# Layer 1's input projection as four pairs of blocks with seven products each, their weights prepared in layer 0

## The chip, the cores and the metric

The kernel runs on one core of one Trainium2 chip. The metric is the device time of one execution in microseconds. Five engines work side by side, each on its own queue in a fixed order: TensorE (PE, with its weight loads shown as PEld), VectorE (DVE), ScalarE (ACT), GpSimd (POOL) and SyncE (SP), which here issues nearly all transfers (DMA).

## The reference, cut to what is computed

Two layers over x of 1024 tokens by 1024 channels, all in float32:

```python
for l in range(DEPTH):
    h = rmsnorm(x, attn_norm[l])
    proj = h @ w_in[l]                       # 1024 x 1952
    (c_q, c_kv, k_r, g_b, g_c, u_conv, u_pool, q_sw, k_sw, v_sw) = split(proj)
    y_a = mla_attention(c_q, c_kv, k_r, ...)         # causal, 4 heads, rotary key
    y_b = short_gated_conv(g_b, g_c, u_conv, ...)    # g_b * conv3(g_c * u)
    y_c = multiscale_pool(u_pool, ...)
    y_d = swa_sink_attention(q_sw, k_sw, v_sw, ...)  # window 128
    x = x + groupnorm([y_a, y_b, y_c, y_d]) @ w_o[l]
    gate, up = split(rmsnorm(x, ffn_norm[l]) @ w_gate_up[l])
    x = x + (silu(gate) * up) @ w_down[l]
return rmsnorm(x, final_norm)
```

## The kernel before

**Layout.** Channels lie on the 128 partitions and tokens along the free side, in two halves of 512 (t = 0 and 1). The channels of x make NK = 8 slices of 128. `w_in` is cut into blocks of 128 output columns: 2, 3 and 0 are the window attention's k, v and first q, 1 its second q, 4 to 9 the convolution's u, c and b for two channel groups, 10 to 12 the latent queries and keys, 13 and 14 the pool. A narrow block for the rotary key comes by itself.

**Arithmetic.** Each float32 operand is split into a high part (rounded by a cast on ScalarE, `split`, L286, or L218 for weights) and a low part (the remainder, on VectorE, L287 or L219). A product of two such numbers takes three matmuls, `mm3` (L275): high x high, high x low, low x high. A matmul is 128 x 128 by 128 x 512.

**Stages of a layer.** Input projection and mixers, attention and output projection, gate-up, down projection. In layer 0 the products of the down projection run from 808.6 us of the span to about 1021, and then layer 1's input projection begins. Gate-up and the down projection already use a scheme of seven products: a product of 2 x 2 blocks is made of seven block products instead of eight, from sums of the blocks. For the weights of the down projection those sums are made during gate-up by `dn_sums` (L164), which loads w_down, adds and stores to the DRAM tensor `qd`. The down projection has 28 units (seven products times four), each of 11 x 3 = 33 matmuls. For a unit the weights (`dn_raw`, L1455) are loaded from `in_w_dn` or `qd`, two pieces of 1024 and 384 columns, and split (`dn_weights`); for each of the seven products the activations (`dn_acts_raw`, L1472 and L1475) are loaded from `ad` and split. `evac` (L1642) adds a unit's sums onto x, which is loaded from `xr`, and `done` splits x times the next layer's gain into `hh`, which feeds the next input projection, and stores x to `xs`.

**Input projection.** `project` takes the next block's weights (`weights`: load L210, then the split) and makes for each half of the tokens 8 slices x 3 = 24 matmuls. The result is multiplied with r, the reciprocal norm of each token, when it is taken from PSUM (L360 and others). In layer 1 blocks 2, 3 and 0 come first.

**Memory and order.** Nearly all tiles live in N_U = 47 slots of two halves of 128 x 512, handed out in order; a tile `u_7577` is the 7577th one made, and a load into a slot waits until the readers of the slot's last tile are done. The order of each engine's queue is made by `order_engines` when the program is built: a table of numbers, MOVED, shifts each step's rank, and `arrange` then lists the steps. The engines keep that order on the chip. SP's transfers wait in the same way, one behind the other.

Of the kernel before, what the change touches and what calls it, by code (L numbers as in the profile page):

```python
# [18 lines left out]
P = 128  # L19
# [24 lines left out]
WARM = 10  # L44

# [70 lines left out]
def trunk_kernel(ctx: ExitStack, tc: tile.TileContext, ins, out):  # L116
# [26 lines left out]
    nffn = cpool.tile([P, L * NK], F32, name="nffn")  # L143
    act.preload_act_table_set("natural_log_exp_and_others")
# [6 lines left out]
    qd = dpool.tile([4, P, NK // 2 * NG * P], F32, name="qd")  # L151

    def dn_sums(l):
# [15 lines left out]

    PS_BUFS = {"mm": 2, "s": 3, "t": 2, "pv": 1}  # L170
# [6 lines left out]
        "dc": deque(["t", "t", "mm", "mm"]),  # L177
    }
# [14 lines left out]
    ring = deque()  # L193

    def ring_next():

        while len(ring) >= 2:
            ring_drop()
        ring.append((R.pair(), R.pair()))
        return ring[-1]  # L200

# [19 lines left out]

    def rope_weights(l):
# [12 lines left out]
    stream, fetched = deque(), deque()  # L235
# [4 lines left out]
    def expect_layer(l):  # L240
        for m in ((2, 3, 0) if l else ()) + (4, 5, 6, 1, 13, 14, 10, 11, 12, None, 7, 8, 9):
            if m is None:
                expect(rope_weights, l)
            else:
# [4 lines left out]
    def ahead():  # L249
        if stream and not fetched:  # L250
            f, args = stream.popleft()
            fetched.append(f(*args))
# [108 lines left out]

    def pcol(l, c, rows=slice(0, P)):
        return par[rows, l * PC_N + c : l * PC_N + c + 1]
# [80 lines left out]

    last_silu = None
    for l in range(L):
        if l == 0:
            expect_layer(0)
        sums = dn_sums(l)

# [17 lines left out]
        def project():  # L468
# [3 lines left out]
            return pp  # L472
# [12 lines left out]
        def swa_q(m, pp):  # L485
            for t in range(2):
                f = tmp()
                dve.scalar_tensor_tensor(
                    out=f, in0=pp[t], scalar=0.125, in1=r_of(t), op0=ALU.mult, op1=ALU.mult
                )  # L490
# [9 lines left out]
                )  # L500

        if l == 0:
# [6 lines left out]
            pk = [pk0, proj(wk, 1)]  # L509
            pv_ = [pv0, proj(wv, 1, "s")]  # L510
            enter_norm(0)
            pq = [pq0, proj(w, 1, "t")]
            enter_norm(1)
            dve.tensor_copy(e_r, cst[:, CC_E : CC_E + P])
            for i in range(L):
                for o, c, n in ((nsink, PC_SINK, 8), (nffn, PC_FFN, NK)):
# [7 lines left out]
        else:  # L524
            wk = take()
            pk = [proj(wk, 0, "s")]
            wv = take()
            pv_ = [proj(wv, 0, "s")]
            pk.append(proj(wk, 1))
            pv_.append(proj(wv, 1, "s"))  # L530
            w = take()
            pq = [proj(w, 0, "s"), proj(w, 1, "t")]
        ahead()
        kk = [[R.pair(), R.pair()] for _ in range(2)]
        for t in range(2):
            f = tmp()
            mul_to(f, pk[t], r_of(t))
            for g, own, oth in ((0, hd, tl), (1, tl, hd)):
# [4 lines left out]
                dve.tensor_tensor(out=k2[oth], in0=f[own], in1=rd(k1[own]), op=ALU.subtract)  # L543
        vs = [[R.half(), R.half()] for _ in range(2)]
        for t in range(2):
            f = tmp()
            mul_to(f, pv_[t], r_of(t))
# [12 lines left out]

        swa_q(0, pq)
# [151 lines left out]
        def conv(ct):  # L713

            z = F.pair()
            pp = project()
            for t in range(2):
                mul_to(F.ap(z + t), pp[t], r_of(t))
            yield
            pp = project()  # L720
            for t in range(2):
                f = tmp()
                mul_to(f, pp[t], r_of(t))
                mul_to(F.ap(z + t), F.ap(z + t), f)
            ac = F.pair()
# [14 lines left out]
            pp = project()  # L740
            for t in range(2):
                f = tmp()
                mul_to(f, pp[t], r_of(t))
                mul_to(F.ap(ac + t), F.ap(ac + t), f)
            y["b"][ct] = [ac, ac + 1]
            yield

        for _ in conv(0):
            swa_some(3)
        swa_q(1, project())  # L750
# [8 lines left out]
        nextp = project()  # L759
        for ct in range(2):  # L760
            pp = nextp
            u, a, b = F.pair(), F.pair(), F.pair()
            uf, af, bf = F.ap2(u), F.ap2(a), F.ap2(b)
            for t in range(2):
                mul_to(F.ap(u + t), pp[t], r_of(t))
            nextp = project()
# [51 lines left out]
        for m in range(2):  # L818
            pp = project() if m else nextp
            for t in range(2):  # L820
                f = tmp()
                mul_to(f, pp[t], r_of(t))
# [6 lines left out]
        pp = project()  # L829
        for t in range(2):  # L830
            s = F.half()
            mul_to(F.ap(s), pp[t], r_of(t))
# [302 lines left out]
        def minus(o, a, b):  # L1135
            dve.scalar_tensor_tensor(
                out=o, in0=a, scalar=-1.0, in1=b, op0=ALU.mult, op1=ALU.subtract
            )

# [106 lines left out]
        def product(p, w, b, start=True, stop=True, again=False):  # L1246
            terms = []
            for j, hl in enumerate(b):
                ks = slice(j * P, (j + 1) * P)
                terms.append((w[0][:, ks], w[1][:, ks], R.ap(hl[0]), R.ap(hl[1])))  # L1250
            mm3(p, terms, start, stop, again)

        def onto(p, w, b):

            product(p, w, b, False, True, True)

# [28 lines left out]
        for n, (h, t) in enumerate(steps):  # L1285
# [28 lines left out]
            if n == 6:  # L1314
# [12 lines left out]
                for k in range(2):  # L1327
                    src = ins["w_o"][l, 4 * k : 4 * k + 4, :, : 2 * P]
# [57 lines left out]

        def neg_mul(o, a, b):
            dve.scalar_tensor_tensor(
                out=o, in0=a, scalar=-1.0, in1=b, op0=ALU.mult, op1=ALU.mult
            )  # L1390
# [140 lines left out]
        for f in range(NPL, NFF):  # L1531
# [12 lines left out]
            if not end:  # L1544
                next(sums, None)
            gate = w.gate
# [73 lines left out]
        def done(d, t):  # L1620
# [7 lines left out]
            if not last:  # L1628
                F.free(x[d][t])

# [24 lines left out]
        for n, (c, m) in enumerate(units):  # L1655
            if n < 5:
                for _ in range(3):
                    next(sums, None)
            if n + 2 < len(units):
# [12 lines left out]
            w = wq.popleft()  # L1672
            i = n // NM
# [27 lines left out]
            elif c == B22:  # L1701
                done(2 * m, 1)
                if m == 0:
                    expect_layer(l + 1)
                    ahead()
# [81 lines left out]
DRAM_TILES = {"xs", "xp", "xr", "qd", "out"} | {f"ad{n}" for n in range(7)}  # L1787
BUFS = {"ps_mm": 2, "ps_s": 3, "ps_t": 2, "ps_pv": 1, "te": 2, "tn": 3, "tp": 3, "vraw": 2, "vhi": 2, "vlo": 2, "sm1": 16, "sm4": 16, "sm8": 16, "sm16": 2}
# [764 lines left out]
```

## Time and profile before

| | |
|---|---|
| three runs | 2051.62, 2052.42, 2052.92 us; median 2052.42 |
| span of the profiled execution, first to last instruction | 2050.3 us, 2.1 below that median |
| mean granted TensorE clock | 0.998 |
| PE, PEld, DVE, ACT, POOL busy | 2034.3, 1675.7, 1599.7, 981.9, 7.9 us |
| transfers | 289.74 MB, mean 141 GB/s |

A time of its own for the profiled execution is not listed beside its span. Rows of groups read: line, engine, operation, output and inputs, shapes, count, then busy time and mean duration of one in ns, then the idle time before it and what ended that. Rows of waits read: who, for whom, total us, times, longest. Rows of stretches: start and end in us, length, busy time and count of each engine, granted clock, share of the 16 transfer engines, GB/s. Rows of transfers: kind, count, size, median us from issue to landing.

### The profile page before, as it was taken

The numbers are of one execution on the slowest core, as the hardware profiler recorded it, in microseconds if no ns is written. First come the engines' busy times: TensorE is split into PE (matmuls) and PEld (weight loads), VectorE is DVE, ScalarE is ACT, GpSimd is POOL, SyncE is SP. The second block draws the span as 40 slices with busy tenths as digits, with TensorE's granted clock in tenths as the row PEclk, the third lists the DMA queues.
The fourth block names the chain that finished last, engine by engine and source line by source line (L and its number), as shares of the span: only waits on it lengthen the run. The fifth ranks groups of instructions, "written<-read, shape, count | busy, mean of one in ns | idle before, by whom it ended". The sixth has DMA issues, their size and how long they took to land. (4 is left out here: it accounts for less than half of the span.)

```text
span 2050.3 us, 26022 instructions
## 1 busy us (share of the span) xinstructions
PE 2034.3 (99%) x9418; PEld 1675.7 (82%) x9418; DVE 1599.7 (78%) x2742; ACT 981.9 (48%) x1713; POOL 7.9 (0%) x38
## 2 busy tenths in 40 slices
PE   9999999999999999999999999999999999999997
PEld 7887888888878888888888878877888888888887
DVE  7889988998778887556566898889987877876555
ACT  6447666653333335344443576657433333354342
POOL 0000000000000000000000000000000000000000
PEclk9999999999999999999999999999999999999999
DMA  5020223355445547766411102142564544487552
GB/s 182 24 73 21 74 84 111 113 190 176 161 143 186 172 154 232 240 236 221 139 37 44 47 22 93 57 146 101 175 203 151 179 160 146 167 295 242 172 195 86
DMA packets 149249, 289.74 MB, mean 141 GB/s; under 512 B 12672, under 2 KB 72064, under 8 KB 149120
## 3 DMA queue, kind: packets, MB, share of 16 engines
q1 hardware_dynamic: 148976, 288.03, 41.8%
q8 instruction: 74, 1.21, 0.2%
q14 instruction: 55, 0.45, 0.1%
q10 hardware_dynamic: 144, 0.05, 0.0%
HBM read 204.67 MB, written 83.36 MB: 140 GB/s over the span
## 5 line engine op out<-in xcount | busy, mean ns | idle before, releaser
L275 PE MATMUL ps_mm<-u,u 128*128 128x512 f32 (+1 forms) x3376 | 858.6, 389 | 0.3 <-DVE u L287 0.2
L275 PEld LDWEIGHTS ps_mm<-u,u 128*128 128x128 f32 x3376 | 617.0, 188 | 130.0 <-issue 5.9
L275 PE MATMUL ps_s<-u,u 128*128 128x512 f32 x2666 | 686.0, 390 | 2.4 <-DVE u L287 2.3
L275 PEld LDWEIGHTS ps_s<-u,u 128*128 128x128 f32 x2666 | 499.4, 188 | 109.6 <-DVE u L287 3.2
L286 ACT CAST u<-u 128x1024 fp32r<-128x1024 f32 (+2 forms) x385 | 334.7, 891 | 451.9 <-PE ps_mm L275 92.5
L287 DVE TENSOR_TENSOR u<-u,u 128x1024 fp32r<-128x1024 f32 (+2 forms) x385 | 387.6, 1023 | 161.3 <-ACT u L286 134.6
L275 PE MATMUL ps_t<-u,u 128*128 128x512 f32 (+1 forms) x1122 | 287.5, 379 | 1.0 <-DVE u L1642 1.0
L275 PEld LDWEIGHTS ps_t<-u,u 128*128 128x128 f32 x1122 | 203.5, 188 | 42.6 <-issue 1.7
L275 PE MATMUL ps_pv<-u,u 128*128 128x512 f32 x744 | 214.7, 390 | 0.5 <-ACT u L286 0.5
L275 PEld LDWEIGHTS ps_pv<-u,u 128*128 128x128 f32 x744 | 139.4, 188 | 30.4 <-ACT u L286 0.9
L289 ACT ACTIVATE u<-u,par 128x512 fp32r<-128x512 f32 x100 | 69.0, 717 | 40.5 <-DVE u L360 14.0
L1394 ACT ACTIVATE tp<-tp 128x512 f32<-128x512 f32 x84 | 52.8, 631 | 71.5 <-DVE tp L360 71.4
L164 DVE TENSOR_TENSOR u<-u 128x256 f32<-128x256 f32 x176 | 73.4, 421 | 14.9 <-DMA u<-in_w_dn 12.7
L286 ACT CAST u<-ps_t 128x512 fp32r<-128x512 f32 (+3 forms) x128 | 60.9, 501 | 50.2 <-PE ps_t L1036 28.0
L287 DVE TENSOR_TENSOR u<-ps_t,u 128x512 fp32r<-128x512 f32 (+3 forms) x128 | 71.7, 576 | 13.9 <-ACT u L286 12.7
L1262 ACT COPY tn<-ps_s 128x512 f32<-128x512 f32 x64 | 37.4, 584 | 79.5 <-PE ps_s L275 77.3
L290 DVE SCALAR_TENSOR_TENSOR u<-u,par,u 128x512 fp32r<-128x512 f32 x100 | 72.5, 746 | 3.1 <-ACT u L289 3.0
L321 ACT ACTIVATE tn<-u 128x512 f32<-128x512 f32 (+1 forms) x93 | 52.9, 592 | 35.4 <-DVE u L1642 25.7
L1395 DVE TENSOR_TENSOR tp<-tp,u 128x512 f32<-128x512 f32 x84 | 57.2, 686 | 11.8 <-ACT tp L1394 11.6
L219 DVE TENSOR_TENSOR u<-u,u 128x1024 fp32r<-128x1024 f32 (+1 forms) x43 | 48.1, 1119 | 16.0 <-PE ps_mm L275 6.4
L218 ACT CAST u<-u 128x1024 fp32r<-128x1024 f32 (+1 forms) x43 | 41.8, 971 | 39.0 <-DMA u<-in_w_in 26.7
L360 DVE TENSOR_TENSOR tp<-tp,u 128x512 f32<-128x512 f32 x84 | 57.3, 685 | 0.5
(196 smaller groups left out, 2007.3 us busy)
## 6 DMA issues: line engine op xcount, KB each, us to landing
u<-in_w_gu SPq DMA_DIRECT2D x88, 512.0 KB, 3.9
ad<-u SPq DMA_DIRECT2D x154, 256.0 KB, 2.1
u<-ad SPq DMA_DIRECT2D x70, 512.0 KB, 5.0
u<-in_w_dn SPq DMA_DIRECT2D x68, 512.0 KB, 3.7
qd<-u SPq DMA_DIRECT2D x44, 512.0 KB, 3.2
u<-qd SPq DMA_DIRECT2D x32, 512.0 KB, 5.2
u<-in_w_in SPq DMA_DIRECT2D x27, 512.0 KB, 3.5
u<-in_xT SPq DMA_DIRECT2D x32, 256.0 KB, 5.0
```

What stands on the lines that cost most here:

```text
L164: dve.tensor_tensor(out=o, in0=o, in1=u, op=ALU.add)
L218: act.copy(hi[:, :n], raw[:, :n])
L219: dve.tensor_tensor(out=lo[:, :n], in0=raw[:, :n], in1=rd(hi[:, :n]), op=ALU.subtract)
L275: pe.matmul(o, w, r, start=start and k == 0 and i == 0, stop=stop and k == n - 1 and i == 2, skip_group_check=again,)
L286: act.copy(hi, f)
L287: dve.tensor_tensor(out=lo, in0=f, in1=rd(hi), op=ALU.subtract)
L289: act.activation(hi, f, AF.Copy, scale=gain)
L290: dve.scalar_tensor_tensor(out=lo, in0=f, scalar=gain, in1=rd(hi), op0=ALU.mult, op1=ALU.subtract)
L321: act.activation(q, f, AF.Square)
L360: dve.tensor_tensor(out=o, in0=a, in1=b, op=ALU.mult)
L1394: last_silu = act.activation(g, g, AF.Silu)
L1395: dve.tensor_tensor(out=g, in0=g, in1=r, op=ALU.mult)
```

## The change

**Pairs.** In layer 1 the blocks (2, 3), (0, 5), (4, 6) and (1, 13) are worked as pairs. With the slices of x taken as even and odd (four each), the halves of the tokens and the two blocks of a pair, one pair is a 2 x 2 by 2 x 2 product, made of seven products of 4 slices x 3 = 12 matmuls each: A11 with x's even slices of half 0 (B11), A12 with the odd ones (B21), and S2, S1, S3, S4 and A22 with N2, N1, T3, T4 and B22. `in_round` runs each of the seven for all four pairs before the next, with new VectorE additions (L622, L643, L649) and ScalarE copies (L608) of the partial sums.

**Combinations of x.** `in_combine` makes N1, N2, T3 and T4 for each of four pairs of slices and splits them. It runs in the last quarter of layer 0's down projection, product B22, and needs x again, which is read back from `xs` (`again`, L1887).

**Weights.** The 15 block weights of layer 1 and its w_o are no longer loaded and split in layer 1. In layer 0 `pre_fast` loads the pairs' weights (`in_w_is`, laid out by the host), makes S1 to S4, splits all seven and stores both parts to `fw`; this runs in units 5 to 22 of the down projection. `pre_plain` does the same for the other seven blocks and w_o, without sums, to `pw`: seven sources in gate-up, ten in the down projection. In layer 1 both parts are loaded from there (`fast_weights`, `pre_weights`).

**Mixers.** The convolution takes u as it is and multiplies with the square of r; block 13 and block 5 or 6 are taken from PSUM or their sums earlier; a pair's second block comes with a negative sign.

**Order.** MOVED is new throughout.

```diff
+FAST = ((2, 3), (0, 5), (4, 6), (1, 13))
+PLAIN = (14, 10, 11, 12, 7, 8, 9)
+    fw = [dpool.tile([2, 7, P, HT], F32, name=f"fw{n}") for n in range(len(FAST))]
+    pw = [dpool.tile([2, P, D], F32, name=f"pw{n}") for n in range(N_PRE)]
+    def pre_fast():
+        n = HT // 2
+        for p in range(len(FAST)):
+            for c in range(0, HT, n):
+                cols = slice(c, c + n)
+                def put(k, v, first, m):
+                    v = v[:, : m * n].rearrange("p (b n) -> p b n", b=m)
+                    sp.dma_start(fw[p][k, first : first + m, :, cols].rearrange("b p n -> p b n"), v)
+                i, j = F.pair(), F.pair()
+                raw, lo = F.ap2(i), F.ap2(j)
+                v = raw.rearrange("p (b n) -> p b n", b=4)
+                sp.dma_start(v, ins["w_is"][p, :, :, cols].rearrange("b p n -> p b n"))
+                yield
+                h, hi = parted(raw[:, : 3 * n], lo[:, : 3 * n])
+                put(0, hi, A11, 3)
+                put(1, lo, A11, 3)
...
+                for o, u in ((b22, b21), (b21, b11), (b11, b22), (b12, b11)):
+                    dve.tensor_tensor(out=o, in0=o, in1=u, op=ALU.add)
+                yield
+                h, hi = parted(raw, raw)
+                put(0, hi, S2, 4)
+                put(1, raw, S2, 4)
...
+    def pre_plain():
+        src = [(ins["w_in"][1, m], D) for m in PLAIN]
+        src += [(ins["w_o"][1, d, :, 2 * P :], 6 * P) for d in range(NK)]
...
+        for o, (w, n) in zip(pw, src):
+            i = F.pair()
+            raw = F.ap2(i)[:, :n]
+            sp.dma_start(raw..., w)
+            yield
+            h, hi = parted(raw, raw)
+            sp.dma_start(o[0, :, :n], hi)
+            sp.dma_start(o[1, :, :n], raw)
...
+        if l:
+            for k in (A11, A12, S2, S1, S3, S4, A22):
+                for p in range(len(FAST)):
+                    expect(fast_weights, p, k)
...
-            expect(weights, ins["w_o"][l, d, :, 2 * P :], 6 * P)
+            if l:
+                expect(pre_weights, len(PLAIN) + d, 6 * P)
...
+    def in_combine(j, x):
+        (a0, b0), (a1, b1) = [[F.ap(x[2 * j + n][t]) for t in range(2)] for n in range(2)]
...
+        act.activation(v0, b0, AF.Copy, scale=g0)
+        act.activation(v1, b1, AF.Copy, scale=g1)
+        dve.scalar_tensor_tensor(out=n1, in0=a0, scalar=g0, in1=v0, op0=ALU.mult, op1=ALU.subtract)
+        minus(n2, n1, v1)
+        hq[N2][j] = half_split(n2)
+        hq[N1][j] = half_split(n1)
+        dve.tensor_tensor(out=t3, in0=v1, in1=v0, op=ALU.subtract)
+        hq[T3][j] = half_split(t3)
+        dve.scalar_tensor_tensor(out=t4, in0=a1, scalar=natt[:, n : n + 1], in1=n2, op0=ALU.mult, op1=ALU.subtract)
+        hq[T4][j] = half_split(t4)
...
+    def in_round(made):
+        for p in range(n):
+            pa.append(ps("fa"))
+            product(pa[p], take(), hq[B11])
+            k1.append(kept(pa[p]))
+            ahead()
+        for p in range(n):
+            pc = ps("fc")
+            product(pc, take(), hq[B21])
+            c = F.ap(k1[p])
+            dve.tensor_tensor(out=c, in0=pc, in1=c, op=ALU.add)
+            ahead()
+        for p in range(n):
+            onto(pa[p], take(), hq[N2])
+            k2.append(kept(pa[p]))
+            ahead()
...
+            if 4 < f < NFF - 2:
+                next(pre_p, None)
...
             if n < 5:
                 for _ in range(3):
                     next(sums, None)
+            elif n < 23:
+                for _ in range(2):
+                    next(pre_f, None)
+            next(pre_p, None)
...
+            if not last and c == B22:
+                for d in (2 * m - 2, 2 * m - 1) if m else ():
+                    again(x, d, 0, 1)
...
+                for k in () if last else range(max(m - 1, 0), m if m < NM - 1 else NM):
+                    in_combine(k, x)
```

**SP's queue in the middle of layer 0's down projection.** Before, in the fourth of the seven products (`ad_93`), the queue holds loads of activations, of weights (`qd`) and of x (`xr`):

```order
L1455 DMA u_7799<-qd 128x1024
L1669 DMA u_7848<-xr 128x512
L1455 DMA u_7848<-qd 128x384
L1455 DMA u_7903<-qd 128x1024
L1455 DMA u_7060<-qd 128x384
L1669 DMA u_7628<-xr 128x512
L1472 DMA u_7897<-ad_93 128x1024
L1472 DMA u_7948<-ad_93 128x1024
```

Now, at the same product, with `fw_98` and `pw_113` the stores of a pair's and of a plain source's parts, and `in_w_is` and `in_w_o` the loads for the next:

```order
L195 DMA fw_98<-u_7833 128x3x256
L232 DMA pw_113<-u_7907 128x768
L195 DMA fw_98<-u_7831 128x3x256
L233 DMA pw_113<-u_7838 128x768
L229 DMA u_7977<-in_w_o 128x768
L195 DMA fw_98<-u_7902 128x4x256
L1705 DMA u_7979<-qd 128x1024
L195 DMA fw_98<-u_7830 128x4x256
L200 DMA u_7969<-in_w_is 128x4x256
L1933 DMA u_7915<-xr 128x512
```

Seven of ten rows are new, and the loads of the down projection stand between them.

**SP's queue late in that projection, now.** Product T4 (`in_w_dn`) gives way to B22 (`ad_91` are its activations):

```order
L1705 DMA u_8581<-in_w_dn 128x1024
L1877 DMA xs<-u_7915 128x512
L1705 DMA u_8521<-in_w_dn 128x1024
L1722 DMA u_8633<-ad_91 128x1024
L1722 DMA u_8702<-ad_91 128x1024
L1705 DMA u_8651<-in_w_dn 128x1024
```

Between the load of u_7577 (`in_w_dn`, 16 units earlier, where the first stores to `fw` stand) and that of u_8651, both included, the queue holds 125 transfers of 51.4 MB: 28 stores to `fw` (12.85 MB), 14 to `pw` (6.03), loads from `in_w_is` (2.62) and `in_w_o` (2.62), `ad` (11.01), `qd` (8.65), `in_w_dn` (3.41) and `xr` (2.36), and 1.84 MB to `xs`. In TensorE's queue 545 matmuls lie between the last reader of the tile that held u_7577's slot before and the last reader of the tile that held u_8651's, and 53 more end with the first that reads what is split from u_8651.

**TensorE's queue at the start of layer 1.** Before, one block's weights (u_8620 and u_8621, high and low) with the two halves of x, 24 matmuls each into ps_mm and ps_s, and the norm of half 1 (L340) in between:

```order
L275 MATMUL ps_mm<-u_8560,u_8620 128x512 x2
L275 MATMUL ps_mm<-u_8560,u_8621 128x512
L340 MATMUL ps_pv<-u_8778,ones_r 128x512 x2
L275 MATMUL ps_s<-u_8117,u_8620 128x512
L275 MATMUL ps_s<-u_8117,u_8621 128x512
```

Now, right behind the last unit of the down projection (ps_mm), A11 of the first three pairs (u_8901, u_8982, u_9073 come from `fw`):

```order
L372 MATMUL ps_mm<-u_8774,u_8998 128x512 x3
L437 MATMUL ps_pv<-u_8985,ones_r 128x512 x2
L372 MATMUL ps_s<-u_8359,u_8901 128x512
L372 MATMUL ps_s<-u_8359,u_8982 128x512
L372 MATMUL ps_s<-u_8359,u_9073 128x512 x3
```

No cast or subtraction stands between these loads and the matmuls any more. 83 matmuls, the two of the norm among them, lie between the last unit and the first that reads N2 of the last pair of slices. On VectorE, 21 instructions follow that unit's `evac` up to the one that makes that operand's low part.

More of the change, by code (lines that the diff above doesn't have):

```diff
@@ L246, in expect_layer, with ahead @@
         for d in range(NK):
-            expect(weights, ins["w_o"][l, d, :, 2 * P :], 6 * P)
-    def ahead():
-        if stream and not fetched:
+            if l:
+                expect(pre_weights, len(PLAIN) + d, 6 * P)
+            else:
+                expect(weights, ins["w_o"][l, d, :, 2 * P :], 6 * P)
+    def ahead(n=3):
+        while stream and len(fetched) < (n if stream[0][0] is fast_weights else 1):
             f, args = stream.popleft()
@@ L443, in finish, with product, onto, minus @@
                 sp.dma_start(o[:, :, cols].rearrange("d p n -> p d n"), both)
+    def product(p, w, b, start=True, stop=True, again=False):
+        terms = []
+        for j, hl in enumerate(b):
+            ks = slice(j * P, (j + 1) * P)
+            terms.append((w[0][:, ks], w[1][:, ks], R.ap(hl[0]), R.ap(hl[1])))
+        mm3(p, terms, start, stop, again)
+    def onto(p, w, b):
+        product(p, w, b, False, True, True)
+    def minus(o, a, b):
+        dve.scalar_tensor_tensor(
+            out=o, in0=a, scalar=-1.0, in1=b, op0=ALU.mult, op1=ALU.subtract
+        )
@@ new lines, in trunk_kernel, with __init__, __getitem__, drop @@
+    class Out:
+        def __init__(self, aps, neg=False, held=()):
+            self.aps, self.neg, self.held = aps, neg, held
+        def __getitem__(self, t):
+            return self.aps[t]
+        def drop(self):
+            for i in self.held:
+                F.free(i)
+    def in_round(made):
+        def spent(c):
+            for hl in hq[c]:
+                for i in hl:
+                    R.free(i)
+        def kept(p):
+            i = F.half()
+            act.copy(F.ap(i), p)
+            return i
+        n = len(FAST)
+        pa, k1, k2, k5 = [], [], [], []
+        for p in range(n):
[13 more added lines that the diff above has]
+            ahead()
+        spent(N2)
+        pc = []
+        for p in range(n):
+            pc.append(ps("fc"))
+            product(pc[p], take(), hq[N1])
+            k5.append(kept(pc[p]))
+            ahead()
+        spent(N1)
+        for p, (a, b) in enumerate(FAST):
+            made[a] = Out([F.ap(k1[p]), F.ap(k2[p])], False, (k1[p], k2[p]))
+            made[b] = Out([pa[p], F.ap(k5[p])], True, (k5[p],))
+        yield
+        for p in range(n):
+            onto(pa[p], take(), hq[T3])
+            c = F.ap(k5[p])
+            dve.tensor_tensor(out=c, in0=pa[p], in1=c, op=ALU.add)
+            ahead()
+        spent(T3)
+        for p in range(n):
+            onto(pc[p], take(), hq[B22])
+            c = F.ap(k2[p])
+            dve.tensor_tensor(out=c, in0=pc[p], in1=c, op=ALU.add)
+            ahead()
+        yield
+        for p in range(n):
+            onto(pa[p], take(), hq[T4])
+            ahead()
+        spent(T4)
@@ L523, in trunk_kernel, with k_split @@
                     )
[L524 to L535, printed above, removed]
+        def k_split(pk, t):
             f = tmp()
-            mul_to(f, pk[t], r_of(t))
+            times_r(f, pk, t)
             for g, own, oth in ((0, hd, tl), (1, tl, hd)):
@@ L543, in trunk_kernel @@
                 dve.tensor_tensor(out=k2[oth], in0=f[own], in1=rd(k1[own]), op=ALU.subtract)
+        if l == 0:
+            ahead()
+            kk = [[R.pair(), R.pair()] for _ in range(2)]
+            for t in range(2):
+                k_split(pk, t)
+        else:
+            rnd = in_round(made)
+            next(rnd)
+            kk = [[R.pair(), R.pair()] for _ in range(2)]
+            k_split(made[2], 0)
+            next(rnd)
+            k_split(made[2], 1)
+            project(2).drop()
+            swa_q(0, project(0))
+            for _ in rnd:
+                pass
+            pv_ = project(3)
         vs = [[R.half(), R.half()] for _ in range(2)]
@@ L713, in conv @@
         def conv(ct):
+            u0, c0, b0 = (4, 5, 6) if ct == 0 else (7, 8, 9)
             z = F.pair()
[L716 to L720, printed above, removed]
+            u = project(u0)
+            if not u.held:
+                for t in range(2):
+                    act.copy(F.ap(z + t), u[t])
+                u = Out([F.ap(z + t) for t in range(2)])
+                yield
+            g = project(c0)
             for t in range(2):
                 f = tmp()
-                mul_to(f, pp[t], r_of(t))
-                mul_to(F.ap(z + t), F.ap(z + t), f)
+                act.activation(f, r_of(t), AF.Square)
+                if g.neg:
+                    neg_mul(F.ap(z + t), g[t], u[t])
+                else:
+                    mul_to(F.ap(z + t), g[t], u[t])
+                mul_to(F.ap(z + t), F.ap(z + t), f)
+            u.drop()
+            g.drop()
+            if b0 in made:
+                b = F.pair()
+                g = project(b0)
+                for t in range(2):
+                    times_r(F.ap(b + t), g, t)
+                g.drop()
+            else:
+                b = None
             ac = F.pair()
@@ L739, in conv @@
             yield
-            pp = project()
+            pp = project(b0) if b is None else None
             for t in range(2):
-                f = tmp()
-                mul_to(f, pp[t], r_of(t))
+                f = tmp() if pp else F.ap(b + t)
+                if pp:
+                    times_r(f, pp, t)
                 mul_to(F.ap(ac + t), F.ap(ac + t), f)
+            if b is not None:
+                F.free_pair(b)
             y["b"][ct] = [ac, ac + 1]
             yield
-        for _ in conv(0):
+        conv0 = conv(0)
+        if l:
+            next(conv0)
             swa_some(3)
-        swa_q(1, project())
+            zp = F.pair()
+            pp = project(13)
+            for t in range(2):
+                times_r(F.ap(zp + t), pp, t)
+            pp.drop()
+            swa_some(3)
+        for _ in conv0:
+            swa_some(3)
+        swa_q(1, project(1))
         ytiles("c")
@@ L1244, in split4 @@
                 F.free_pair(self.raw[1])
[L1246 to L1255, printed above, removed]
         def blocks(hl, n):
@@ L1627, in done, with again @@
                 ss.add(t, a[:, cols], cols)
-            if not last:
+            if not last and (d, t) != (NK - 2, 1):
                 F.free(x[d][t])
+        def again(x, d, *ts):
+            i = F.pair() if len(ts) > 1 else F.half()
+            cols = slice(ts[0] * HT, (ts[-1] + 1) * HT)
+            sp.dma_start(F.ap2(i) if len(ts) > 1 else F.ap(i), xs[d][:, cols])
+            for t in ts:
+                x[d][t] = i + t - ts[0]
         def evac(c, m, p, cols=whole):
```

147 lines of the change are left out of this document (113 added, 34 removed), and 723 rows, old and new, of the table MOVED.

## The prediction

> **What bounds the kernel now.** I read the page's busy times and slices first, then TensorE's own waits, then its instructions in order of time for the cost of one matmul, then the stretches of layer 0's down projection, where the change puts its new work, and last the durations of single operations.
>
> ```profile
> span 2050.3 us, 26022 instructions
> PE 2034.3 (99%) x9418; PEld 1675.7 (82%) x9418; DVE 1599.7 (78%) x2742; ACT 981.9 (48%) x1713; POOL 7.9 (0%) x38
> PE   9999999999999999999999999999999999999997
> DVE  7889988998778887556566898889987877876555
> PEclk9999999999999999999999999999999999999999
> DMA  5020223355445547766411102142564544487552
> GB/s 182 24 73 21 74 84 111 113 190 176 161 143 186 172 154 232 240 236 221 139 37 44 47 22 93 57 146 101 175 203 151 179 160 146 167 295 242 172 195 86
> ```
>
> TensorE is busy in every slice at full clock. Its waits, in the view that lists them for one engine, add up to 6.9 us:
>
> ```profile
> PE ps_s L275 <- DVE u L287: 2.3, 2, 1.7
> PE ps_mm L275 <- DVE u L913: 1.3, 4, 0.6
> PE ps_pv L505 <- DVE ones L138: 1.1, 1, 1.1
> PE ps_t L275 <- DVE u L1642: 1.0, 2, 0.5
> PE ps_s L345 <- ACT tn L321: 0.5, 1, 0.5
> PE ps_pv L275 <- ACT u L286: 0.5, 1, 0.5
> PE ps_mm L275 <- DVE u L287: 0.2, 1, 0.2
> ```
>
> So the time is the number of matmuls times their spacing, and only fewer matmuls or new waits can move it. The spacing is in TensorE's order of time at the end of layer 0, a train of 84:
>
> ```profile
> 1006.25 19.20 PE L275 MATMUL ps_mm<-u,u 128*128 128x512 f32 x84
> 1025.29 5.83 PE L275 MATMUL ps_s<-u,u 128*128 128x512 f32 x25
> L275 PE MATMUL ps_mm<-u,u 128*128 128x512 f32 x3244 | 842.3, 393 | 0.3 <-DVE u L287 0.2
> L275 PEld LDWEIGHTS ps_mm<-u,u 128*128 128x128 f32 x3376 | 617.0, 188 | 130.0 <-issue 5.9 <-DVE u L287 0.9 <-ACT tn L1262 0.6
> ```
>
> (19.20 - 0.393) / 83 = 0.2266 us. The Trainium skill, Perfetto Trace Analysis, section Identifying the Most-Contended Engine, calls the busy share of matmuls a poor measure and asks for that of the weight loads; by its 82% TensorE would have room, and fewer matmuls might be worth less than their share. The rows do not bear this out: 188 ns of each 226.6 ns spacing are 83%, so the missing 18% is a piece of every spacing and not a stretch in which work is waited for.
>
> **The matmuls.** Eight of layer 1's blocks took 8 blocks x 2 halves x 8 slices x 3 terms = 384 matmuls; as four pairs they take 4 pairs x 7 products x 4 slices x 3 terms = 336. TensorE's queue is otherwise the same in kind and number. 48 x 0.2266 = 10.9 us less, all on the path, since the engine they leave is never idle there. This is the only gain.
>
> **The transfers in layer 0's down projection.** Here the rows are stretches of time: the down projection (its products begin at 808.6, its loads at about 777), its last fifth, layer 1's start, and then the densest stretches of transfer in the trace.
>
> ```profile
> 775.00:1025.00 250.00, 250.00 (x1104) 207.02 (x1104) 155.97 (x192) 115.15 (x151) 0.00 (x0) 1.00 0.66 218
> 975.00:1025.00 50.00, 50.00 (x222) 41.38 (x221) 30.04 (x40) 23.14 (x35) 0.00 (x0) 1.00 0.44 134
> 1025.00:1250.00 225.00, 224.51 (x1074) 182.94 (x1074) 177.00 (x370) 119.76 (x259) 0.35 (x2) 1.00 0.13 41
> 3.00:23.00 20.00, 19.88 (x85) 15.73 (x85) 17.71 (x32) 18.26 (x30) 0.00 (x0) 1.00 1.03 376
> 10.00:20.00 10.00, 10.00 (x46) 8.29 (x45) 9.71 (x16) 9.95 (x18) 0.00 (x0) 1.00 1.06 402
> 874.00:884.00 10.00, 10.00 (x46) 8.29 (x45) 9.05 (x10) 7.90 (x11) 0.00 (x0) 1.00 1.03 405
> 1818.00:1848.00 30.00, 30.00 (x134) 24.75 (x133) 24.57 (x31) 15.35 (x18) 0.00 (x0) 1.00 0.95 333
> ...
> 442.00:446.00 4.00, 1.00 0.98 329
> 628.00:632.00 4.00, 1.00 0.96 358
> ...
> u<-in_w_dn SPq DMA_DIRECT2D x68, 512.0 KB, 3.7
> L287 DVE TENSOR_TENSOR u<-u,u 128x1024 fp32r<-128x1024 f32 x256 | 309.7, 1221 | 116.0 <-ACT u L286 89.9 <-PE ps_s L275 9.2 <-PE ps_pv L275 5.1
> L286 ACT CAST u<-u 128x1024 fp32r<-128x1024 f32 x256 | 265.3, 1051 | 281.6 <-DMA u<-ad 78.8 <-PE ps_s L275 46.8 <-DMA ad<-u 32.3
> ```
>
> The last three columns are the granted clock, the transfer share and GB/s (the two short rows give no engines). Before, 250 us move 218 GB/s, 54.5 MB. The change adds 4.2 MB of loads and 14.7 MB of stores for the pairs, 4.2 MB and 8.4 MB for the ten plain blocks that fall here (seven lie in gate-up), and 3.9 MB of x read back: 35 MB, to 90 MB, 360 GB/s as a mean. It is not even. In SP's queue of the changed kernel, between the load of u_7577 and that of u_8651 (both down weights), stand 51.4 MB. The slot of the first is given up by a matmul after which 545 follow until the slot of the second is given up: 545 x 0.2266 = 123.5 us, so the order asks for 416 GB/s. From there it is 53 matmuls, 12.0 us, until TensorE needs u_8651; its landing takes 3.7 us and its split 1.05 on ScalarE and 1.22 on VectorE, so it may be 6.0 us late at no cost. The wait is therefore 51.4 MB / R - 123.5 - 6.0.
>
> R is not shown over so long a stretch. Bounds: 405 GB/s (ten full microseconds with loads and stores mixed, 874 to 884) gives 126.9 us and no wait; 333 (30 us at share 0.95, with gaps in which nothing was queued) gives 154.4 us and a wait of 24.9 us. Between them stands 376 over 20 us at share 1.03, that is a queue that never ran dry: 136.7 us, a wait of 7.2 us. The mix of loads and stores is that of 874-884, but 16.5 MB of it, 32%, go in pieces of 256 numbers, 1 KB, as gate-up's sums do in 442-446 and 628-632: 329 / 0.98 = 336 and 358 / 0.96 = 373 GB/s at full share, 354 between them. 1 / (0.32 / 354 + 0.68 / 405) = 387; I take 385: 133.5 us, a wait of 4.0 us. Later the order asks for less, and the delay does not grow.
>
> The Trainium skill, HBM Reference, Specifications (TRN2), gives a core some 358 GB/s as its share when both cores of a pair stream, and about 425 alone. With 358 the sum would be 51.4 / 0.358 = 143.6 us, a wait of 14.1 us, which is rival two below. The rows at 402 and 405 lie above that share, and one core runs, so the trace bears out the larger figure for 10 us at a time.
>
> The stores stand in the one queue on SP: each waits for ScalarE's or VectorE's half of a split, and every load of down weights and activations behind it waits too; where several microseconds of issued transfers lie ahead, such a hold is hidden, so I add nothing for it.
>
> **VectorE and ScalarE.** Durations:
>
> ```profile
> L164 DVE TENSOR_TENSOR u<-u 128x256 f32<-128x256 f32 x176 | 73.4, 421 | 14.9 <-DMA u<-in_w_dn 12.7
> L219 DVE TENSOR_TENSOR u<-u,u 128x1024 fp32r<-128x1024 f32 x27 | 32.9, 1220 | 15.2 <-PE ps_mm L275 6.4 <-PE ps_pv L340 3.7 <-PE ps_t L275 2.9
> L219 DVE TENSOR_TENSOR u<-u,u 128x768 fp32r<-128x768 f32 x16 | 15.2, 950 | 0.7 <-ACT u L218 0.6
> L287 DVE TENSOR_TENSOR u<-tp,u 128x512 fp32r<-128x512 f32 x32 | 21.3, 682 | 0.3 <-ACT u L286 0.3
> L1149 DVE SCALAR_TENSOR_TENSOR tp<-u,par,te 128x512 f32<-128x512 f32 x8 | 5.9, 743 | 0.0
> L1642 DVE TENSOR_TENSOR u<-u,ps_s 128x512 f32<-128x512 f32 x24 | 16.4, 682 | 13.4 <-PE ps_s L275 13.4
> ```
>
> Weights of the pairs: 8 rounds x (0.95 + 4 x 0.421 + 1.22) = 30.8 us of VectorE; plain blocks 8 x 0.95 + 2 x 1.22 = 10.0; the four combinations of x 4 x (2 x 0.743 + 6 x 0.682) = 22.3. With 156.0 that is 219 of 250 us, so this engine still fits, but the last combinations fall at the end. From the last eviction of layer 0 to the lower half of N2's last slice VectorE has 21 instructions, 21 x 0.69 = 14.5 us; TensorE meanwhile has 83 matmuls, 18.8 us. The cover is 4.3 us. In 975-1025 VectorE was busy 30.0 us; with 22.3 and a last round of 3.9 that is 56 in 50, so it arrives some microseconds behind, and I put 0.5 us here, bounds 0 and 5. Seven plain blocks, spread over gate-up, cost 7 x 1.22 = 8.5 us there, where the page's slices leave VectorE about a fifth idle.
>
> In layer 1, 15 + 2 splits of 1.22 and eight of 0.95 leave VectorE (28.3 us) and twelve additions of 0.68 come (8.2). Nothing is gained, as TensorE lost only 0.5 us in 225 there. Twice as many bytes of weights meet a transfer share of 0.13. The new order of the rest, the squares in the convolution and the negated gains I put at nothing: the waits there are 6.9 us in all, and may shift by a microsecond either way.
>
> **Sum.** -10.9 + 4.0 + 0.5 = -6.4 us. The profiled span of 2050.3 becomes 2043.9; the median of the runs, 2052.42, lies 2.1 above that span and goes to 2046.0.
>
> **Rivals.** One: transfers run at 400 or more throughout, waits 0 to 2 us, 2041.5 to 2043.5. For it speak the two full 10 us rows; against it that nothing so long is shown. Two, the other sign: the queue falls behind through the second half of the down projection and TensorE waits for its weights. It decides at 51.4 MB / R = 123.5 + 6.0 + 10.9, R = 366 GB/s; at 350 the time is 2059, at 333 it is 2067. Every slice of the page lies below 300, which speaks for it; that no slice was full (a share below 0.9 in each) speaks against. Three: VectorE is late at layer 1's entry, TensorE waits up to 5 us before N2, 2046.5 to 2051 with the transfers as I took them; the 56 in 50 speaks for it, the 18.8 us of products that need no combination against it. That no matmul is saved is excluded by the queue.
>
> **Chances.** 0.2% is 4.1 us, about what a measurement of this kernel can tell from no change. Waits under 2 us: 0.27; 2 to 6.8 us (my forecast, 2043.5 to 2048.3): 0.40; 6.8 to 15 us, within 0.2% of before: 0.20; more, rival two in full: 0.13. So faster 0.67, same 0.20, slower 0.13. The range reaches from every wait gone and a microsecond of the old ones too, 2040.5, to 2055.5, R of about 359; it leaves out rival two's far part.
>
> **What would show it.** 48 matmuls fewer; transfers at 370 to 405 GB/s with share near 1 from about 830 to 960; TensorE's waits in the down projection on L383 and L384 (the splits), 2 to 6 us, around 945 to 975, behind loads of in_w_dn and ad; waits at layer 1's entry below 1 us. A share below 0.9 in that stretch with waits of 10 us would mean that SP's queue was held by stores and not by the wire; waits before N2 on L384 alone would put the loss on VectorE.

## The result: 37.6 us slower, and the profile after

| | runs | median, us |
|---|---|---|
| before | 4 | 2052.33 |
| after | 4 | 2089.89 (2086.88 to 2093.16) |

The ratio is 1.0183, with a 95% interval of 1.0168 to 1.0197. The profiled execution of after has a span of 2086.2 us; its time, 2088.02 us, lies 1.9 below the median. First the page's busy times, matmul count and slices of the changed kernel:

```profile
span 2086.2 us, 26359 instructions
PE 2047.3 (98%) x9370; PEld 1660.0 (80%) x9370; DVE 1639.9 (79%) x2820; ACT 1013.4 (49%) x1771; POOL 8.0 (0%) x38
PE   9999999999999999999999999999999999999998
DMA  4020223254656567999772314243553554387552
GB/s 179 23 71 21 80 86 113 97 183 163 222 179 214 196 215 245 380 386 382 261 241 93 107 54 121 65 162 112 188 201 134 192 169 138 135 291 247 176 183 91
```

The matmuls are 48 fewer (9370 for 9418), and the three full slices at 380 to 386 GB/s are layer 0's down projection. A TensorE that is busy in every tenth hides the loss; its waits in after show it, 29 us against 6.9:

```profile
PE ps_pv L372 <- ACT u L383: 6.1, 5, 2.0
PE ps_s L372 <- ACT u L383: 5.9, 3, 5.0
PE ps_t L372 <- ACT u L383: 4.6, 6, 2.1
PE ps_t L372 <- DMA u<-fw: 2.7, 2, 1.4
PE ps_pv L372 <- DVE u L384: 2.0, 2, 1.5
PE ps_s L372 <- DVE u L384: 2.0, 4, 0.7
PE ps_s L372 <- ACT tn L1512: 1.3, 2, 1.0
```

L383 and L384 are the high and low part of a split, 20.6 us in these rows. Their waits come singly and far apart: nine in layer 0's gate-up, two long ones in its down projection, most of the rest in layer 1's gate-up and down projection. The 29 us are not the whole loss, which in this execution is 47 us when the gain of 10.9 is allowed for: matmuls that start late by less than the view lists, and stretches at a lower clock (last section), come on top. Where the loss lies is read best from the number of matmuls that a stretch holds (the x behind PE): 378 us at 0.2266 have room for 1668, 175 us for 772 to 774. Gate-up and down projection of layer 0 before, then the same in after:

```profile
430.00:808.00 378.00, 376.28 (x1660) 311.00 (x1659) 308.88 (x476) 136.29 (x187) 0.00 (x0) 1.00 0.52 176
808.00:1021.00 213.00, 213.00 (x942) 176.36 (x941) 128.56 (x157) 96.95 (x126) 0.00 (x0) 1.00 0.64 212
```

```profile
430.00:808.00 378.00, 369.38 (x1593) 296.14 (x1593) 304.04 (x467) 135.57 (x184) 0.00 (x0) 1.00 0.58 193
825.00:1000.00 175.00, 167.81 (x730) 137.75 (x728) 129.10 (x167) 91.48 (x111) 0.00 (x0) 0.98 1.04 385
1000.00:1025.00 25.00, 24.80 (x103) 20.02 (x102) 19.44 (x27) 14.47 (x21) 0.00 (x0) 0.93 0.77 265
```

Gate-up lost 67 matmuls' time, 15 us, with a transfer share of 0.58. To place the rest, the start times of matmuls were compared at equal progress, from both traces: how much later than before the same amount of TensorE's work is begun, as the step over each stage (the runs further down are in it already). In layer 1 the 48 matmuls are allowed for, so that -10.9 is their gain. Each row is one execution, which can lie off its run's median: that of stores16 is 8.6 us above, that of after_order 3.0 and that of before_early 2.0 below, the others 1.9 or less:

| run | to 430 | layer 0 gate-up | layer 0 down | layer 1 projection, attention | layer 1 gate-up, down | sum |
|---|---|---|---|---|---|---|
| after | 3.3 | 15.8 | 11.4 | -6.3 | 11.8 | 36.0 |
| stores16 | 3.0 | 10.9 | 0.2 | 0.1 | 16.6 | 30.8 |
| idle | 3.9 | 8.3 | 0.2 | -6.0 | 13.7 | 20.1 |
| after_twice | 2.6 | 12.1 | 1.7 | -3.5 | 5.3 | 18.2 |
| after_search | 3.1 | 8.7 | 3.1 | -8.4 | 3.3 | 9.8 |
| after_order | 1.3 | 1.3 | 2.4 | -9.7 | 2.6 | -2.1 |
| after_best | 1.1 | 2.0 | 2.7 | -9.4 | 3.4 | -0.2 |
| idle_best | 2.9 | 1.3 | 1.4 | -10.3 | 3.3 | -1.4 |
| after_last | 1.1 | 4.7 | 1.8 | -11.0 | 2.8 | -0.6 |
| before_early | 3.7 | 1.0 | 1.8 | 2.1 | -0.9 | 7.7 |
| before_order | 0.8 | -2.0 | 0.0 | 0.0 | -0.7 | -1.8 |

The second last column of the first row was not expected: layer 1's gate-up and down projections, whose code the change does not touch, lose 11.8 us.

How one of the waits comes about, the longest, in after's order of time (all engines, then TensorE alone):

```profile
914.11 1.46 SPq L1722 DMA_DIRECT2D u<-ad  x2
915.92 0.32 SPq L233 DMA_DIRECT2D pw<-u  x1
916.42 0.37 SPq L195 DMA_DIRECT2D fw<-u  x1
918.65 2.94 SPq L195 DMA_DIRECT2D fw<-u  x3
921.04 1.04 ACT L383 CAST u<-u 128x1024 fp32r<-128x1024 f32 x1 [0.68 <-DMA u<-ad]
922.37 1.99 ACT L383 CAST u<-u 128x1024 fp32r<-128x1024 f32 x2 [0.28 <-DMA u<-ad]
```

```profile
916.78 2.65 PE L372 MATMUL ps_mm<-u,u 128*128 128x512 f32 x11
924.41 1.22 PE L372 MATMUL ps_s<-u,u 128*128 128x512 f32 x2 [4.97 <-ACT u L383]
925.43 1.91 PE L372 MATMUL ps_mm<-u,u 128*128 128x512 f32 x4
927.13 8.24 PE L372 MATMUL ps_s<-u,u 128*128 128x512 f32 x33
```

Two loads of activations, issued from 914.11, land 6.9 and 7.0 us after their issue, at 921.02 and 922.29; two casts follow at once, a third behind them, and TensorE has stood still for 4.97 us. The wait names ScalarE, but a transfer was late. Late by what? The kernel's planner fixes the order by a formula for each transfer:

```python
wire = max(t + (1000 if v.stores else 1400), wire) + v.size / 400.0
v.end = wire + 345 if v.stores else wire + 470 + v.size / 1885.0
```

With the issue times of the traces put in, the 783 transfers on SP before land 0.63 us later than it says as a mean, the 919 after 1.05. In after the median is 0.2 us where nothing is ahead in the queue by the formula, and 1.9 us, with a tenth above 3.2, where 0.5 us of transfers or more are ahead; before, 0.1 and 1.5. The change made the second kind more frequent: 348 for 180. The Trainium skill, DMA: Bandwidth & Descriptors, section Latency and other measured facts, gives the HBM's access latency as 0.2 us on average and 2 us at high load. That is not the same quantity: the figures here are lateness over a formula that has a fixed time of its own. They are alike in size, but no run here separates the latency from the rest.

### The profile page after: what moved, and what is told of

It is laid out like the page before. It is cut to its first block, busy times and chain, and to the rows that moved or that the text cites. A ratio compares the mean times of both kernels' runs of the same rounds, so it can differ in the third digit from the quotient of the medians.

```text
span 2086.2 us, 26359 instructions
## 1 busy us (share of the span) xinstructions
PE 2047.3 (98%) x9370; PEld 1660.0 (80%) x9370; DVE 1639.9 (79%) x2820; ACT 1013.4 (49%) x1771; POOL 8.0 (0%) x38
## 4 chain that ended last, share of the span: by engine, by line
PE 77%; DMA 10%; DVE 8%; ACT 3%; issue 2%; SPq 0%; DVEq 0%; ACTq 0%
PE ps_mm L372 30%; PE ps_s L372 20%; PE ps_t L372 10%; PE ps_pv L372 7%; DVE u L384 2%; PE ps_pv L1314 2%; DMA u<-qd 1%; PE ps_t L1302 1%; ACT u L383 1%; DMA u<-in_w_dn 1%; DMA pw<-u 1%; DMA u<-ad 1%; DMA ad<-u 1%; PE ps_t L442 1%; DMA fw<-u 1%
## 5 line engine op out<-in xcount | busy, mean ns | idle before, releaser
L372 PE MATMUL ps_mm<-u,u 128*128 128x512 f32 (+1 forms) x3184 | 809.3, 390 | 1.7 <-DMA u<-pw 0.6
L372 PEld LDWEIGHTS ps_mm<-u,u 128*128 128x128 f32 x3184 | 580.4, 189 | 126.3 <-issue 5.5
L372 PEld LDWEIGHTS ps_s<-u,u 128*128 128x128 f32 x2714 | 505.7, 188 | 131.2 <-ACT u L383 9.1
L383 ACT CAST u<-u 128x1024 fp32r<-128x1024 f32 (+2 forms) x385 | 335.0, 890 | 423.8 <-PE ps_mm L372 91.1
L384 DVE TENSOR_TENSOR u<-u,u 128x1024 fp32r<-128x1024 f32 (+2 forms) x385 | 386.9, 1021 | 153.0 <-ACT u L383 114.9
L372 PEld LDWEIGHTS ps_t<-u,u 128*128 128x128 f32 x1170 | 211.3, 188 | 53.2 <-ACT u L383 7.9
L372 PE MATMUL ps_pv<-u,u 128*128 128x512 f32 x792 | 202.4, 395 | 8.2 <-ACT u L383 6.1
L372 PEld LDWEIGHTS ps_pv<-u,u 128*128 128x128 f32 x792 | 148.0, 190 | 45.6 <-ACT u L383 8.6
L383 ACT CAST u<-ps_t 128x512 fp32r<-128x512 f32 (+3 forms) x128 | 60.4, 500 | 57.4 <-PE ps_t L1302 43.6
L384 DVE TENSOR_TENSOR u<-ps_t,u 128x512 fp32r<-128x512 f32 (+3 forms) x128 | 71.5, 576 | 17.0 <-ACT u L383 15.6
L1314 PE MATMUL ps_pv<-u,u 128*128 128x512 f32 (+2 forms) x184 | 54.0, 365 | 0.0
L183 DVE TENSOR_TENSOR u<-u,u 128x1024 f32<-128x1024 f32 (+1 forms) x33 | 35.9, 1093 | 20.1 <-ACT u L182 19.9
```

The source lines that it names most:

```text
L372: pe.matmul(o, w, r, start=start and k == 0 and i == 0, stop=stop and k == n - 1 and i == 2, skip_group_check=again,)
L383: act.copy(hi, f)
L384: dve.tensor_tensor(out=lo, in0=f, in1=rd(hi), op=ALU.subtract)
L1314: pe.matmul(py[:, c0:], v_of(j, h), R.ap(s)[:, c0:], start=j == 0 and n == 0, stop=j == nj - 1 and n == 1,)
```

## The experiments

Two theories. **Order**: the new order lets loads land in time by the formula only; on the chip they land later, and the loss follows from the order, wherever in the kernel. **Work** (first called bytes): the preparation's transfers, casts and subtractions hold TensorE up under any order.

**Three to begin with.** `after_twice` and `before_twice` have the same instructions as their kernels and a second pass of the planner:

```diff
-    for queue in arrange(steps).values():
+    arrange(steps)
+    first = {v: v.start for v in steps}
+    late = dict(land=800.0, rate=383.0, sig=5.0, dve=1.005)
+    for queue in arrange(steps, lambda v: first[v], **late).values():
```

`land` is added to each landing, `rate` takes the place of 400, `sig` is added to each semaphore's delay. `stores16` keeps after's order and cuts the stores (`r` is P // 16 but for the first pair and source):

```diff
+                    r = P if p == 0 else P // 16
-                    sp.dma_start(fw[p][k, first : first + m, :, cols]..., v)
+                    sp.dma_start(fw[p][k, first : first + m, :r, cols]..., v[:r])
```

> The changed kernel, all its work kept. Only the order is made anew: the planner lists the steps as before, then once more with each step's start of the first pass as its rank, and with transfers taken to land 0.8 us later, at 383 instead of 400 GB/s, semaphores 5 ns later and VectorE 0.5% slower. Theory order (the new order leaves loads no time to be late, and late loads cost in every stage): the waits of layer 0's gate-up (16 us against before), of its down projection (11) and of layer 1's gate-up and down projections (11.5) mostly go, 2050 to 2065. Theory bytes (65 MB more transfers and 40 us more of VectorE's work in layer 0 cost under any order): layer 0's 27 us stay, 2075 to 2090.

Measured: 2070.19 us, ratio 1.0086 (1.0071 to 1.0101): 20 us gone with not a byte less, short of what order expected, below what bytes did. With the same bytes at 394 GB/s layer 0's down projection now keeps TensorE fed, 767 matmuls in 175 us for 730; gate-up is still short, 1606. The two stretches in after_twice:

```profile
430.00:808.00 378.00, 370.35 (x1606) 297.95 (x1606) 307.04 (x469) 136.97 (x186) 0.00 (x0) 1.00 0.59 195
825.00:1000.00 175.00, 174.13 (x767) 143.28 (x766) 135.62 (x176) 95.53 (x118) 0.00 (x0) 1.00 1.05 394
```

> The kernel before with the same second pass of the planner. Control for what a second pass gives by itself. Theory order: before has few waits (6.9 us), so little is to be had, 2046 to 2054. Theory bytes says nothing of it: 2052, within 4 us. If it falls by 15 us or more, the second pass is a gain that has nothing to do with the change.

Measured: 2054.30 us, 1.0007 (0.9999 to 1.0016). The second pass gives the kernel before nothing.

> The changed kernel with its order kept word for word (the planner is given the old sizes), but the stores of three of the four pairs and of 16 of the 17 plain sources write 8 of 128 partitions, and layer 1 loads all its weights from the pair and the source that are still whole: 26 MB fewer stored, 22 of it in the down projection, all else the same in number and place. Its results are not the reference's. Theory bytes: layer 0's loss goes, in gate-up as in the down projection, 2058 to 2066. Theory order: only the down projection's 11 us come back, while gate-up's 16 and layer 1's 11.5 stay, 2074 to 2081.

Measured: 2074.33 us, 1.0109 (1.0088 to 1.0130); its profiled execution took 2082.9, so its row in the table sums to 8.6 us more than the median would, and in which stage is not known. In that row it is as order expected: the down projection's 11 us are back (0.2), gate-up keeps 10.9 of 15.8. But 4.9 us of gate-up came back with the stores too, which order had not expected.

**What does the order alone cost, and can it be had in the kernel before?** `idle` takes after's order as lists and cuts the preparation's work on every engine to 32 columns:

```diff
+                w = FEW if p else n
-                sp.dma_start(v, ins["w_is"][p, :, :, cols]...)
+                sp.dma_start(v[:, :, :w], ins["w_is"][p, :, :, cols][:, :, :w]...)
+        if not whole:
+            raw, lo = raw[:, :FEW], lo[:, :FEW]
```

`before_early` is `before_twice` with `late = dict(land=-500.0)`. `after_search` is `after_twice` with `land=1200.0` and 56 shifts.

> The changed kernel's order, word for word on every engine, with nearly all of the preparation's work in layer 0 taken out but none of its instructions: for three of the four pairs and 16 of the 17 plain sources the loads, casts, sums, subtractions and stores take 32 columns instead of 256 to 1024, and layer 1 loads its weights from the pair and the source that are still whole. Its results are not the reference's. What is left of the change there is its order and the 48 matmuls fewer. Theory order: gate-up's loss stays at 8 to 16 us, layer 1's at 10 or more, 2064 to 2078. Theory work (bytes, or VectorE's and ScalarE's added work, hold TensorE up): layer 0's loss goes and with it most of the rest, 2041 to 2052.

Measured: 2073.06 us, 1.0098 (1.0082 to 1.0113), inside order's range. With next to nothing prepared in layer 0, TensorE still waits for the halves of splits that were always there, here L394. The longest rows of its waits, then the two stretches:

```profile
PE ps_pv L383 <- ACT u L394: 4.5, 4, 1.9
PE ps_t L383 <- ACT u L394: 3.4, 3, 1.7
PE ps_t L383 <- DMA u<-fw: 1.9, 2, 1.6
```

```profile
430.00:808.00 378.00, 372.89 (x1624) 300.79 (x1622) 303.27 (x475) 132.92 (x188) 0.00 (x0) 1.00 0.52 172
825.00:1000.00 175.00, 175.00 (x774) 144.72 (x772) 113.59 (x178) 80.61 (x119) 0.00 (x0) 1.00 0.79 262
```

Gate-up is 44 matmuls short of 1668 in it. (`idle` still moves 318 MB, for 353 in after and 288 before: one pair, x read back and layer 1's loads of prepared weights remain.) The preparation's work under this order is then worth 2089.9 - 2073.1 = 16.8 us. What is left stands 32 us above 2052.3 - 10.9; layer 1's part of the change is still in it, but layer 1's largest share, 13.7, lies in its untouched stages.

> The converse: the kernel before, not one instruction or byte more, with a second pass of the planner as in before_twice (which gave 2054.3) in which transfers are taken to land 0.5 us earlier than the planner's own numbers have it, not later. Theory order: an order that leaves loads less time loses by that alone, in the same small waits, 2058 to 2075. Theory work: 2052 to 2056, the order is indifferent while the work is the same.

Measured: 2061.90 us, 1.0043 (1.0030 to 1.0057). The kernel before, not changed but for an order that asks for earlier landings, loses 9 us.

> The changed kernel, all its work kept, with the second pass of the planner taking transfers to land 1.2 us later (after_twice: 0.8 us, 2070.2), and 56 shifts of single steps found by a search against the same numbers. Theory order: more slack takes away more of the small waits, 2050 to 2060. Theory work: what after_twice left is the price of the work and the bytes, 2066 to 2074.

Measured: 2061.42 us, 1.0040 (1.0027 to 1.0052), just past the upper end of order's range and below work's. More slack helped again, but gate-up kept 8.7 us.

**How far does it go?** `after_order` and `before_order` have their queues written out as lists, found by a search that draws each landing from those in the traces; `after_best` carries it on, and `idle_best` is `idle` in the order of `after_best`:

```diff
-    for queue in arrange(steps).values():
+    for ranks in order.values():
+        queue = [steps[r] for r in ranks]
```

> The changed kernel, all its work kept, in an order written out as lists, found by a longer search against transfers that land as late, and as unevenly, as the traces show (in the traces they land the later the more is queued: 0.2 us over the planner's number in the median with nothing ahead, 1 to 2.3 us with more than 0.5 us of transfers ahead). Theory order: the waits fall further, 2046 to 2056, with gate-up's loss below 6 us (10.7 in after_search). Theory work: gate-up's 10 us have been there under all four orders so far and stay, 2058 to 2064.

Measured: 2052.93 us, 0.9999 (0.9990 to 1.0008). All 37 us are gone with all the work kept, and gate-up's loss is 1.3 us, with more transfers in it (208 GB/s) than in after (193). Nor do its loads land sooner: against the same formula its 919 transfers are 1.26 us late as a mean, for 1.05 in after. The order is what makes this lateness cheap. The largest rows of TensorE's waits, each now 1.5 us or less, and the stretches:

```profile
PE ps_s L374 <- ACT u L385: 1.5, 2, 0.8
PE ps_pv L732 <- DVE ones L145: 1.1, 1, 1.1
PE ps_s L374 <- ACT tn L1514: 1.0, 2, 0.7
```

```profile
430.00:808.00 378.00, 377.73 (x1655) 307.64 (x1654) 316.95 (x484) 143.59 (x196) 0.00 (x0) 1.00 0.62 208
825.00:1000.00 175.00, 173.40 (x763) 142.53 (x762) 132.98 (x172) 94.59 (x118) 0.00 (x0) 1.00 1.02 382
```

> The kernel before in an order found by the same search, the control for after_order: what a searched order is worth without the change. Theory order: before has few small waits to lose, 2044 to 2052. If it gains as much as after_order does against the changed kernel's own order, the search is the gain and the change is not held up by its order in particular; a gain of 8 us or less against 37 says that it is.

Measured: 2050.26 us, 0.9988 (0.9979 to 0.9996): the search is worth 2.8 us to the kernel before, and 37 to the changed one.

> The changed kernel, all its work kept, with the search of after_order (2052.9) carried on against landings as that run's own trace has them. Theory order: some of the 8 us of waits that after_order still had over the kernel before (2 up to gate-up, 1.3 in gate-up, 2.4 in layer 0's down projection, 1.8 in layer 1's gate-up) go, 2045 to 2051, faster than before. Theory work: they are the work's own and stay, 2051 to 2055.

Measured: 2051.82 us, 0.9992 (0.9983 to 1.0001), no difference from before that the runs can tell. Work's range.

> The order of after_best, word for word, with the preparation's loads, casts, sums and stores cut to 32 columns for three of four pairs and 16 of 17 plain sources, as in idle (2073.1 against the changed kernel's 2089.9). Its results are not the reference's. What it saves against after_best is the price of the work itself under an order made for late landings. Theory order: 1 to 4 us. Theory work: as much as under the change's own order, 12 us or more.

Measured: 2049.61 us, 0.9986 (0.9977 to 0.9995). The whole preparation costs 2.2 us under this order, for 16.8 under after's.

> The changed kernel, all its work kept, in a third searched order. In the traces of after_order and after_best most of what is left is matmuls that start 3 to 100 ns late, singly, behind weight loads whose operand was written in the last 0.2 us; this search prices an operand that is written later than 0.13 us before its matmul, the others didn't. Theory order: some of after_best's (2051.8) remaining 9 us go, 2045 to 2050, faster than the kernel before. If it is 2050 to 2054, either the search has come to its end or what is left is the change's own.

Measured: 2053.41 us, 1.0005 (0.9996 to 1.0014). It did not help: layer 1's projection has the whole gain in it (-11.0), but gate-up loses 4.7. The best order found with the change (0.9992 of before) and the best without it (0.9988) are alike, so no version here beats the kernel before by more than the re-ordered kernel before does.

## Why the prediction was wrong, step by step

**The 48 matmuls: right.** 9370 are recorded, and the stage that they leave is 9.4 to 10.3 us shorter in after_order, after_best and idle_best. After's own order kept 6.3 of it.

**"The new order of the rest, the squares in the convolution and the negated gains I put at nothing": this step failed.** I read before's 6.9 us of waits as a property of the kernel; they were one of its order. `before_early` shows that an order alone moves the unchanged kernel by 9 us, `idle` that 32 of after's 48 us over the forecast gain are there with most of the preparation's work gone, and after_order that 37 of the 48 go with all of the work kept. That late landings are what an order loses by rests on before_early, on the waits that end with a load, and on the gain with each later landing planned for; after_twice and after_search also plan for a lower rate and a slower VectorE, which were not tried singly. My argument that the waits "may shift by a microsecond either way" had no row behind it. The queue before and after could be read beforehand, and the landings in before's trace (0.63 us later than the planner's formula, 1.5 in a full queue) too; an order packed against that formula leaves no room for landings that come later. None of my rivals reached 2089.9; the farthest, 333 GB/s in rival two, gave 2067.

**The transfers in layer 0's down projection, +4.0: the rate right, the wait mis-sized.** The rate was 385 GB/s over 175 us at share 1.04, the very value taken, which the rows behind it (336 to 405) could not promise: after_twice ran at 394 there and after_order at 382. It lies above the 358 that the prediction weighed from the Trainium skill, HBM Reference, Specifications (TRN2). The stage lost 11.4 us; the same bytes lost 1.7 in after_twice and 2.4 in after_order. So the wait is not bytes over rate, as my sum had it, but also where in the queue each load stands and how late it lands with stores around it. The two long waits did lie on L383, but they end at 924 (4.97 us) and 999 (1.86 us), some 20 us ahead of my window and behind it, and 3.8 us more went to slow matmuls after them (last section). Rival two has the sign right and its mechanism wrong: it needed less than 366 GB/s. With the share at 1.04 the transfers did not stand idle behind stores either.

**Gate-up's seven plain blocks, hidden in VectorE's idle fifth: wrong under after's order** (15.8 us, of which stores16 gives 4.9 back and idle 7.5), nearly right under a better one (1.3 with all of them).

**VectorE late at layer 1's entry, +0.5:** it was not VectorE. The rows say DMA u<-fw, 2.7 us, between 1025 and 1250: the loads of the prepared weights, a term that I had put at nothing because the transfer share there was 0.13.

**Still open.** after_best lies 10 us above before less 10.9, and idle_best 8. The table spreads it over all stages, 3.4 of after_best's in layer 1's unchanged ones. In the traces it is mostly single matmuls started a little late: in layer 1's gate-up (1450 to 1815 us) after_best has 165 with a spacing of 229 to 240 ns for 46 before, 0.7 us more, and 32 that are 33 to 100 ns late for 5, 1.8 us more. after_last was made against these and did not help, so whether a better order or the change's own demands explain them is not settled.

## What to carry to other kernels

Where queues are ordered by a plan, a change of the work is also a change of the order, and the plan's margin is part of the kernel: compare the plan's landing times with those in the trace before costing anything at nothing. To tell the two apart, keep the order and take the work out, and keep the work and plan again with later landings; here the first gave back 17 of 48 us and the second 37. Count matmuls per stretch rather than busy time, and look at stages whose code did not change: a loss there points at the order first.

## What the runs showed of the hardware that I had not expected

After the wait of 4.97 us the matmuls start 0.427 us apart ((1.91 - 0.628) / 3, with 0.628 the length of one there). Ten spacings in a row are long, the first 0.591 us, eight of about 0.427 and the last 0.415: 2.2 us on top of the wait. The granted clock (third column from the right) fell in three stretches of after before its last 8 us, each at a wait, and not in a fourth with a wait as long:

```profile
533.00:540.00 7.00, 4.95 (x16) 3.61 (x15) 6.69 (x12) 2.75 (x4) 0.00 (x0) 0.76 1.01 339
921.00:931.00 10.00, 6.59 (x21) 5.30 (x22) 6.96 (x9) 3.98 (x5) 0.00 (x0) 0.66 1.07 396
998.00:1004.00 6.00, 5.34 (x16) 4.21 (x17) 6.00 (x8) 3.52 (x5) 0.00 (x0) 0.72 1.00 366
1872.00:1878.00 6.00, 3.95 (x18) 3.13 (x18) 6.00 (x8) 1.04 (x1) 0.00 (x0) 1.00 0.76 230
```

The waits there were 2.05, 4.97, 1.86 and 2.05 us. In the first three stretches the clock stood at 0.50 from 535.84 to 539.26, 921.55 to 928.38 and 1000.06 to 1003.47 us, that is for 3.41 us or twice that, and at 1.00 around them. The Trainium skill, TensorE: Matmul & The Clock Gate, section Why this matters for your kernels, warns of idle gaps above some 3 us. The second row agrees. In the first and third the clock fell at waits of 2.05 and 1.86 us, and in the fourth it did not at 2.05; what decides between them no run here shows.

A weight load that had to wait cost time though its matmul started on time. In after_best, at 1465.08, one was held some 0.16 us by a semaphore; its matmul followed the one before it at the usual 0.226 us, and the next four 46, 9, 1 and 6 ns late.
